# First norm of a two-layer backbone: leading weight tiles take x times the adaLN scale, with shift and rstd put in afterwards, and every engine in a written order

## The chip, the cores and the metric

The kernel runs on one core of one Trainium2 chip. The metric is the device time of one execution in microseconds (us), and what is compared is the median of several executions. The core has five engines that run side by side, each with its own queue of instructions that it works off in order: TensorE (PE, matrix products; PEld is its loading of weights), VectorE (DVE), ScalarE (ACT), GpSimd (POOL) and SyncE (SP, which here only starts transfers between HBM and the on-chip memory SBUF). Products are accumulated in eight PSUM banks. In this kernel an engine waits for another through semaphores.

## The reference, cut to what matters

The program is a two-layer transformer backbone in float32: two streams of 256 tokens each (latent x and context c), width 1024, each layer a SwiGLU FFN, an attention mixer and a second FFN, every one behind an RMS norm with adaLN (shift, scale, gate). Only the start of layer 0 is touched:

```python
cond_x = jax.nn.silu(c); cond_c = jax.nn.silu(c_ctx)
mx = jnp.split((cond_x @ mod_w[layer] + mod_b[layer])[:, None, :], N_MOD, axis=-1)   # mc with cond_c
y = xf * lax.rsqrt(jnp.mean(xf * xf, axis=-1, keepdims=True) + EPS)                    # rms_norm, then * norm_g
h = y * (1.0 + scale) + shift                                                         # modulate(h, mx[0], mx[1])
g, u = jnp.split(h @ w_in, 2, axis=-1)
return (jax.nn.silu(g) * u) @ w_out
```

Shift and scale are themselves products of a 1024 vector with a 1024x1024 block of `mod_w`, one pair for each stream.

## The kernel before, in words

Everything is held transposed: channels on the 128 partitions, both streams side by side in 512 columns, so x is eight blocks `xs[0..7]` of 128x512. A float32 product is made of three products of float32r halves: the operand is split into a high half (a cast on ACT, line 198) and a low half (a subtraction on DVE, line 199), and `mm3` (lines 226 to 228) adds high x high, high x low, low x high. A weight tile is 128x1024 (eight blocks k, for 128 output channels), so a tile takes 24 products of 128x512. For the FFN, tiles 2f and 2f+1 are the gate and the up part of hidden block f.

The first norm needs shift and scale at once. The matrix block for them is loaded as eight columns (`load_column`, 1 MB each in four transfers of 256 KB), each column with shift and scale of one k. `mod_sums` (line 143) makes 16 small float32 products for a column, ACT copies the result (149), PE turns it (151), and three short DVE instructions (158 to 160) make shift and `(1 + scale) * g`. With these `inputs(k)` makes the normed input of block k: for each stream x times coefficient times rstd on DVE (1049), high half plus shift on ACT (1051), low half on DVE (1052). rstd comes first of all, from the squares of the whole of x (1014, 1018, 1022, 1032, 1036, 1039). The four leading weight tiles (`sl.lead`) are multiplied block by block as the inputs come (`lead_products`); from tile 4 on `Sublayer.products` takes one tile after the other. `fill` (line 88) issues products of ones that nobody reads, 40 at the start and 3 and 5 while columns 0 and 1 are turned.

The order of the instructions on an engine comes from the framework that builds the program, which looks ahead by its own costs; `behind(x)` asks for a place after instruction x. The transfers stand in one SP queue: all of x, then the columns with the four weight tiles between them, then constants, then the first pieces of later work.

Next to the FFN, DVE works through the adaLN vectors of later sublayers (`mod_in_background`, lines 169 and 171: products of 128x1024 blocks with one number per partition, two per block), from hidden block 2 on.

## Time and profile before

| what | value |
|---|---|
| median of three executions | 1690.58 us (1689.67 to 1690.87) |
| profiled execution | 1692.26 us, span of the program in it 1690.5 us |
| PE busy | 1671.4 us, 99% of the span |
| DVE busy | 1076.8 us, 64% |
| ACT busy | 643.1 us, 38% |
| HBM read | 241.16 MB, 143 GB/s over the span |

The rows of the profile name the line of the kernel, engine, operation and tiles. In the timeline a row has the start and the duration in us, and `x4` means that four neighbouring instructions were merged into one row. In brackets stands how long the engine had been idle and what released it. A float32 product of PE shows as two records, so the 16 products of a column are x32. A product of 128x512 shows a duration of about 0.39 us, but the next one starts after 0.23 us, since products are pipelined.

### The profile page before, as it was taken

To read this page: it belongs to the slowest core of one execution; us is meant where nothing else is said; L and a number is where in the kernel's file an instruction comes from. 1 tells how busy PE (TensorE), PEld (TensorE's weight loads), DVE (VectorE), ACT (ScalarE), POOL (GpSimd) and SP (SyncE) were. 2 spreads that over 40 slices of the span, in tenths; PEclk is the share of its full clock that TensorE was granted. 3 is DMA by queue.
4 is the path that set the end of the run, shared out by engine and by line. 5 is a ranking of instruction groups with operands and counts; after the bars stand their busy time and mean duration, and the time that the engine had idled before them with its cause. 6 is when DMAs were issued, how large, how long until landed. Compare 5 with 4: busy or idle time off the path is not lost.

```text
span 1690.5 us, 23440 instructions
## 1 busy us (share of the span) xinstructions
PE 1671.4 (99%) x9294; PEld 1418.6 (84%) x9294; DVE 1076.8 (64%) x1535; ACT 643.1 (38%) x1129; POOL 231.1 (14%) x192
## 2 busy tenths in 40 slices
PE   9999999999999999999999999999999999999997
PEld 7888888888888898888888897888888898889997
DVE  6766687645667568856847365744433367777886
ACT  4421322235556353222222352222222357754444
POOL 0000000004133130000000130000000255132332
PEclk9999999999999999999999999999999999999999
DMA  9645455431211126644645335735332222245553
GB/s 344 221 164 183 166 189 198 159 121 63 88 51 63 63 83 200 204 150 158 205 146 173 106 112 199 238 115 165 114 104 90 98 88 77 71 154 178 173 186 113
DMA packets 71535, 243.75 MB, mean 144 GB/s; under 512 B 8576, under 2 KB 9344, under 8 KB 71424
## 3 DMA queue, kind: packets, MB, share of 16 engines
q1 hardware_dynamic: 70560, 241.54, 43.3%
q8 instruction: 73, 1.20, 0.3%
q10 hardware_dynamic: 864, 0.70, 0.1%
q14 instruction: 38, 0.31, 0.1%
HBM read 241.16 MB, written 1.05 MB: 143 GB/s over the span
## 4 chain that ended last, share of the span: by engine, by line
PE 86%; DMA 5%; POOL 3%; DVE 3%; ACT 2%; issue 1%; ACTq 0%; SPq 0%; DVEq 0%; POOLq 0%
PE bank L226 26%; PE bank L227 26%; PE bank L228 25%; DMA wraw<-in_woutn 3%; POOL wraw L962 3%; DVE wlo L199 2%; ACT whi L198 1%; DMA r2k<-in_modo 1%; PE bank L811 1%; PE bank L842 1%; PE bank L829 1%; PE bank L177 1%; PE bank L956 1%; PE bank L512 1%; PE bank L239 0%
## 5 line engine op out<-in xcount | busy, mean ns | idle before, releaser
L226 PE MATMUL bank<-r2k,whi 128*128 128x512 f32 (+2 forms) x2410 | 859.6, 358 | 0.9 <-ACT small L968 0.9
L227 PE MATMUL bank<-r2k,whi 128*128 128x512 f32 (+2 forms) x2410 | 854.7, 355 | 1.9 <-DVE r2k L202 1.2
L228 PE MATMUL bank<-r2k,wlo 128*128 128x512 f32 (+2 forms) x2410 | 854.3, 355 | 1.1 <-DVE wlo L199 0.9
L198 ACT CAST whi<-wraw 128x1024 fp32r<-128x1024 f32 (+1 forms) x308 | 316.9, 1033 | 840.1 <-PE bank L227 492.5
L226 PEld LDWEIGHTS bank<-r2k,whi 128*128 128x128 f32 x2410 | 455.4, 189 | 79.3 <-ACT whi L198 9.2
L227 PEld LDWEIGHTS bank<-r2k,whi 128*128 128x128 f32 x2410 | 456.3, 189 | 66.7 <-DVE r2k L202 1.9
L228 PEld LDWEIGHTS bank<-r2k,wlo 128*128 128x128 f32 x2410 | 456.2, 189 | 65.5 <-DVE wlo L199 2.0
L199 DVE TENSOR_TENSOR wlo<-wraw,whi 128x1024 fp32r<-128x1024 f32 (+1 forms) x297 | 358.4, 1213 | 109.8 <-ACT whi L198 102.4
L171 DVE SCALAR_TENSOR_TENSOR big<-modraw,conds,big 128x1024 f32<-128x1024 f32 x189 | 233.6, 1280 | 9.5 <-DMA modraw<-in_modw 8.6
L264 POOL TENSOR_TENSOR strip<-strip 128x256 f32<-128x256 f32 x58 | 56.3, 984 | 935.8 <-ACT strip L258 465.6
L366 DVE SCALAR_TENSOR_TENSOR x<-bank,mod,x 128x256 f32<-128x256 f32 x168 | 74.4, 479 | 151.3 <-PE bank L228 149.7
L458 DVE TENSOR_TENSOR tmp<-bank,tmp 128x512 f32<-128x512 f32 x66 | 45.6, 691 | 160.8 <-PE bank L228 158.3
L962 POOL TENSOR_TENSOR wraw<-wraw,gate 128x1024 f32<-128x1024 f32 x22 | 62.1, 2821 | 130.9 <-DMA wraw<-in_woutn 115.3
L956 PE MATMUL bank<-whi,r2k 128*128 128x512 f32 x176 | 58.2, 393 | 3.1 <-DVE r2k L977 1.8
L199 DVE TENSOR_TENSOR r2k<-bank,r2k 128x512 fp32r<-128x512 f32 (+2 forms) x73 | 40.5, 593 | 18.9 <-ACT r2k L198 18.6
L977 DVE TENSOR_TENSOR r2k<-tmp,r2k 128x256 fp32r<-128x256 f32 x22 | 46.6, 2118 | 0.9 <-ACT r2k L976 0.9
L199 DVE TENSOR_TENSOR r2k<-tmp,r2k 128x512 fp32r<-128x512 f32 x66 | 45.2, 685 | 1.4 <-ACT r2k L198 1.4
L198 ACT CAST r2k<-tmp 128x512 fp32r<-128x512 f32 x66 | 41.0, 622 | 11.3 <-DVE tmp L458 11.0
L484 DVE TENSOR_REDUCE small<-bank 128x1 f32<-128x512 f32 (+1 forms) x64 | 37.2, 616 | 10.6 <-PE bank L816 10.3
L956 PEld LDWEIGHTS bank<-whi,r2k 128*128 128x128 f32 x176 | 33.0, 188 | 10.1 <-DVE r2k L977 2.2
L456 ACT ACTIVATE tmp<-bank 128x512 f32<-128x512 f32 x66 | 38.9, 590 | 3.7 <-PE bank L228 3.7
L198 ACT CAST r2k<-bank 128x512 fp32r<-128x512 f32 (+2 forms) x73 | 34.5, 524 | 15.0 <-PE bank L228 9.7
(203 smaller groups left out, 1199.0 us busy)
## 6 DMA issues: line engine op xcount, KB each, us to landing
wraw<-in_win SPq DMA_DIRECT2D x172, 512.0 KB, 3.6
modraw<-in_modw SPq DMA_DIRECT2D x128, 512.0 KB, 4.1
wraw<-in_wout SPq DMA_DIRECT2D x48, 448.0 KB, 3.4
wraw<-in_wout SPq DMA_DIRECT2D x24, 512.0 KB, 4.3
wraw<-in_woutn SPq DMA_DIRECT2D x22, 512.0 KB, 3.5
r2k<-in_modo SPq DMA_DIRECT2D x32, 256.0 KB, 6.0
wraw<-in_mwo SPq DMA_DIRECT2D x8, 512.0 KB, 3.6
wraw<-in_swq SPq DMA_DIRECT2D x8, 512.0 KB, 3.4
```

Of the source, the lines that this page charges most:

```text
L171: nc.vector.scalar_tensor_tensor(acc[s], raw, conds[:, kt, s:s + 1], acc[s], ALU.mult, ALU.add)
L198: nc.scalar.copy(hi, src)
L199: return engine.tensor_tensor(lo, src, hi.bitcast(F32), ALU.subtract)
L226: nc.tensor.matmul(o, lhsT=ah, rhs=bh, start=(i == 0), stop=False)
L227: nc.tensor.matmul(o, lhsT=ah, rhs=bl, start=False, stop=False)
L228: nc.tensor.matmul(o, lhsT=al, rhs=bh, start=False, stop=(i == n - 1))
L264: nc.gpsimd.tensor_tensor(self.parts[0], self.parts[0], q, ALU.add)
L366: nc.vector.scalar_tensor_tensor(xs[d][:, SL[s]], o[:, SL[s]], mod[l][:, s, c:c + 1], xs[d][:, SL[s]], ALU.mult, ALU.add)
L458: nc.vector.tensor_tensor(pr[:, :w], ou[:, :w], sg[:, :w], ALU.mult)
L956: nc.tensor.matmul(acc[i][h], lhsT=gu[a][:, rows], rhs=w[b][:, cols], start=(f == 0 and j == 0), stop=(f == NF - 1 and j == 2))
L962: nc.gpsimd.tensor_tensor(raw, raw, gate, ALU.mult)
L977: nc.vector.tensor_tensor(gu[1], u, gu[0].bitcast(F32), ALU.subtract)
```

## The change

The transfers now stand in this order: x blocks 0 and 1, the scale of columns 0 and 1, two weight tiles; then for each pair of blocks x, scale columns and (twice) a weight tile; then the shift columns pair by pair, with weight tiles 4 and 5 between them. So scale and shift of a pair of columns are two sums of 16 products each in place of two mixed ones: eight sums as before. The result is turned by a product with a 128x4 matrix (`both_halves`) that also adds the halves, in place of a transposition and a DVE addition.

The four leading tiles take z = x times `(1 + scale) * g`, split into halves (`gained_high` on ACT, `gained_low` on DVE): without rstd and without shift. What is missing is put in for hidden blocks 0 and 1: the PSUM result is multiplied by rstd (a factor of each token), and the product of the weight tile with the shift vector (`ends`, 32 small products on PE, a copy, a transposition) is added, in `silu` as its bias and in the up part as a scalar. The normed inputs themselves (`scaled`, `halves`) are still made for the later tiles, after rstd; tiles 4 and 5 (`more`) are multiplied with them. Squares, sums, leading products and inputs are written out in one order, and `queued` holds each of PE, ACT and DVE to that order: an instruction of this stage is placed behind the last one of the stage on its engine. All these instructions carry the line of `queued`, 1035.

```diff
-    for d in range(0, KT, 2):
+    def load_x(d):
         nc.sync.dma_start(x_all[:, d:d + 2], t["xT"][:, d:d + 2])
+    load_x(0)
...
+                if sl.ends is not None and f < 2:
+                    nc.vector.tensor_tensor(sg, og, sl.rstds, ALU.mult)
+                    nc.vector.tensor_tensor(pr, ou, sl.rstds, ALU.mult)
+                    for s in streams:
+                        nc.scalar.activation(sg[:, SL[s]], sg[:, SL[s]], AF.Silu, bias=sl.ends[:, 2 * f, s:s + 1])
+                        nc.vector.scalar_tensor_tensor(pr[:, SL[s]], pr[:, SL[s]], sl.ends[:, 2 * f + 1, s:s + 1], sg[:, SL[s]],
+                                                       ALU.add, ALU.mult)
+                else:
+                    nc.scalar.activation(sg[:, :w], og[:, :w], AF.Silu)
+                    nc.vector.tensor_tensor(pr[:, :w], ou[:, :w], sg[:, :w], ALU.mult)
...
+    scales.append(load_columns(0, 1))
+    load_weight()
+    load_weight()
+    for k in range(2, KT, 2):
+        load_x(k)
+        scales.append(load_columns(k, 1))
+        if k < 6:
+            load_weight()
+    for k in range(0, KT, 2):
+        shifts.append(load_columns(k, 0))
+        if k < 4:
+            more.append(weight_raw(*ffn_specs(0, 0)[len(more) + 4]))
...
+    def queued(engine, f, *args, **kw):
+        with behind(last.get(engine)):
+            last[engine] = f(*args, **kw)
+        return last[engine]
...
+    def gained_low(d):
+        z = zs[d]
+        for s in range(2):
+            dve(nc.vector.scalar_tensor_tensor, z[1][:, SL[s]], xs[d][:, SL[s]], sl.gain(s, d), z[0][:, SL[s]].bitcast(F32),
+                ALU.mult, ALU.subtract)
...
+    sA = sums(scales[0])
+    weight_high(wraws[0], sl.lead)
+    idle(6)
+    v = turn(sA)
+    idle(8)
+    scale_of(0, v)
+    gained_high(0)
+    gained_low(0)
+    weight_low(wraws[0], sl.lead[0])
...
+    sA = sums(scales[3])
+    lead_products((3,), (4,))
+    v = turn(sA)
+    scale_of(6, v)
+    lead_products((3,), (5,))
+    for k in (6, 7):
+        gained_high(k)
+        gained_low(k)
+    sA = sums(shifts[0])
+    scaled(0)
+    lead_products(range(4), (6,))
+    v = turn(sA)
+    shift_of(0, v)
+    scaled(1)
+    sA = sums(shifts[1])
+    weight_high(more[0], more)
+    halves(0)
+    scaled(2)
+    halves(1)
+    weight_low(more[0], more[2])
+    lead_products((0, 1), (7,))
+    v = turn(sA)
+    shift_of(2, v)
+    sA = sums(shifts[2])
+    scaled(3)
+    halves(2)
+    weight_high(more[1], more)
+    scaled(4)
+    halves(3)
+    weight_low(more[1], more[3])
+    del more[:2]
+    lead_products((2, 3), (7,))
+    v = turn(sA)
+    shift_of(4, v)
+    sA = sums(shifts[3])
+    scaled(5)
+    halves(4)
+    scaled(6)
+    halves(5)
+    v = turn(sA)
+    shift_of(6, v)
...
+    def products_of_inputs():
+        for k in range(KT):
+            for wt, o, M in more:
+                mm3(o, sl.terms(wt, M, slice(0, TT)), (k,), KT)
...
+        for k in range(KT):
+            for j in range(4):
+                nc.tensor.matmul(b[32 * j:32 * j + 32, :P], lhsT=shift32[:, k], rhs=wraws[j][:, k * P:(k + 1) * P],
+                                 start=(k == 0), stop=(k == KT - 1), skip_group_check=True)
```

How this stands on the engines, at three places. First PE, from the last column before and from the last shift sum now. In the rows, `32x128 x16` is a sum, `128x512` a product of a weight tile; before:

```order
L143 MATMUL bank<-r2k,cond_124 32x128 x16
L226 MATMUL bank<-r2k,whi 128x512
L227 MATMUL bank<-r2k,whi 128x512
L151 MATMUL bank<-c_ident,tmp 128x128
L228 MATMUL bank<-r2k,wlo 128x512
L226 MATMUL bank<-r2k,whi 128x512
```

Now (`both_halves` is the turning product; the rows of line 1035 end with it, and those of line 217 are tiles 4 and 5):

```order
L1035 MATMUL bank<-both_halves,tmp 128x4
L1035 MATMUL bank<-r2k,cond_121 32x128 x16
L1035 MATMUL bank<-r2k,whi 128x512 x2
L1035 MATMUL bank<-r2k,wlo 128x512
L1035 MATMUL bank<-r2k,whi 128x512 x2
L1035 MATMUL bank<-r2k,wlo 128x512
L1035 MATMUL bank<-both_halves,tmp 128x4
L1035 MATMUL bank<-r2k,cond_121 32x128 x16
L1035 MATMUL bank<-both_halves,tmp 128x4
L217 MATMUL bank<-r2k,whi 128x512
```

Before, products of leading tiles stand between the last sum and its turning product, and go on behind it. Now nothing stands between the last shift sum and its turning product, and all 48 products of tiles 4 and 5 stand behind it.

Second ACT, at the same place. `COPY tmp<-bank 128x128` is the copy of a sum that the turning product waits for, `ACTIVATE r2k<-strip` the high half of a normed input. Before:

```order
L149 COPY tmp<-bank 128x128
L1051 ACTIVATE r2k<-strip,mod_127 128x256 x2
L198 CAST whi<-big 128x1024
L149 COPY tmp<-bank 128x128
L1051 ACTIVATE r2k<-strip,mod_127 128x256 x2
L149 COPY tmp<-bank 128x128
```

Now, from the split of weight tile 4 on:

```order
L1035 CAST whi<-wraw 128x1024
L1035 ACTIVATE r2k<-strip,mod_124 128x256 x4
L1035 COPY tmp<-bank 128x128
L1035 ACTIVATE r2k<-strip,mod_124 128x256 x2
L1035 CAST whi<-wraw 128x1024
L1035 ACTIVATE r2k<-strip,mod_124 128x256 x2
L1035 COPY tmp<-bank 128x128
L189 CAST whi<-wraw 128x1024 x2
```

The copy of the last shift sum stands behind the high halves of inputs 0 to 3 and the high halves of weight tiles 4 and 5, and the high halves of tiles 6 and 7 follow it at once.

Third DVE, from the turning of the first shift pair on. `strip<-x` is x times coefficient times rstd of one stream, `r2k<-strip` a low half, `mod_124<-bank` the shift of a pair:

```order
L1035 TENSOR_TENSOR mod_124<-bank,c_modb 128x2x2
L1035 SCALAR_TENSOR_TENSOR strip<-x,coefA_126,r2k 128x256 x2
L1035 SCALAR_TENSOR_TENSOR r2k<-strip,mod_124,r2k 128x256 x2
L1035 SCALAR_TENSOR_TENSOR strip<-x,coefA_126,r2k 128x256 x2
L1035 SCALAR_TENSOR_TENSOR r2k<-strip,mod_124,r2k 128x256 x2
L1035 TENSOR_TENSOR wlo<-wraw,whi 128x1024
L1035 TENSOR_TENSOR mod_124<-bank,c_modb 128x2x2
L1035 SCALAR_TENSOR_TENSOR strip<-x,coefA_126,r2k 128x256 x2
```

Before, the DVE work of an input stood right behind the coefficient of its own column:

```order
L158 TENSOR_TENSOR mod_127<-bank,c_modb 128x2x2
L159 TENSOR_TENSOR mod_127<-bank,mod_127 128x2x2
L160 SCALAR_TENSOR_TENSOR coefA_129<-mod_127,c_ng 128x2
L1049 SCALAR_TENSOR_TENSOR strip<-x,coefA_129,strip 128x256 x2
L1052 SCALAR_TENSOR_TENSOR r2k<-strip,mod_127,r2k 128x256 x2
```

Now the shift of the second pair stands behind the low halves of the first pair and behind the low half of weight tile 4. All inputs stand behind the 16 low halves of z.

## Prediction

> **What bounds the kernel now.** I read the page first, then the timeline, groups and waits of the first 100 us, where the change is.

> ```profile
> span 1690.5 us, 23440 instructions
> PE 1671.4 (99%) x9294; PEld 1418.6 (84%) x9294; DVE 1076.8 (64%) x1535; ACT 643.1 (38%) x1129; POOL 231.1 (14%) x192
> ```

> PE sets the time. A change can win only PE's waits and its work that no result needs, and it loses whatever wait it puts on PE. The start, in the timeline:

> ```profile
> 1.04 11.66 PE L88 MATMUL bank<-ones 128*128 128x128 f32 x80 [1.04 <-DVE ones L79]
> 12.54 0.95 PE L1022 MATMUL bank<-ones,tmp 128*128 128x1 f32 x8
> 13.42 1.08 PE L143 MATMUL bank<-r2k,cond 128*32 128x128 f32 x32
> 14.43 0.65 PE L1036 MATMUL bank<-c_ident,small 128*128 128x128 f32 x4
> 14.59 0.27 ACT L149 COPY tmp<-bank 128x128 f32<-128x128 f32 x1 [0.80 <-PE bank L143]
> 14.92 0.32 PE L151 MATMUL bank<-c_ident,tmp 128*128 128x128 f32 x1
> 18.12 1.28 PE L88 MATMUL bank<-ones 128*128 128x128 f32 x10
> 19.16 0.48 PE L226 MATMUL bank<-r2k,whi 128*128 128x512 f32 x1
> ```

> The 40 products of ones hold PE until 12.5 us; they stay. The first product of a weight tile starts at 19.16. Then the groups of PE from 19.0 to 52.6 us, and what PE waited for in 12 to 53:

> ```profile
> L226 PE MATMUL bank<-r2k,whi 128*128 128x512 f32 x33 | 13.7, 424 | 0.0
> L227 PE MATMUL bank<-r2k,whi 128*128 128x512 f32 x33 | 13.0, 395 | 0.0
> L228 PE MATMUL bank<-r2k,wlo 128*128 128x512 f32 x32 | 12.6, 405 | 0.0
> L143 PE MATMUL bank<-r2k,cond 128*32 128x128 f32 x192 | 8.1, 277 | 1.0 <-DMA r2k<-in_modo 0.9
> PE bank L143 <- DMA r2k<-in_modo: 1.1, 3, 0.6
> ```

> 98 products have started by 52.6: the 96 of the four leading tiles, and two of tile 4. The waits for columns are 1.1 us in all. How far apart PE starts products, and what a sum costs it:

> ```profile
> 56.46 0.39 PE L226 MATMUL bank<-r2k,whi 128*128 128x512 f32 x1
> 82.30 0.39 PE L226 MATMUL bank<-r2k,whi 128*128 128x512 f32 x1
> 37.43 0.39 PE L228 MATMUL bank<-r2k,wlo 128*128 128x512 f32 x1
> 37.75 1.08 PE L143 MATMUL bank<-r2k,cond 128*32 128x128 f32 x32
> 38.76 0.50 PE L226 MATMUL bank<-r2k,whi 128*128 128x512 f32 x1
> 39.10 0.40 PE L227 MATMUL bank<-r2k,whi 128*128 128x512 f32 x1
> ```

> Between the first two rows lie 38 blocks of three products: 25.84 / 114 = 0.227 us each. From 37.43 to 39.10 two products and a sum are started: 1.67 - 0.45 = 1.2 us for a sum. My yardstick is the end of tile 5, the 144th product. Before it is 52.2 + 48 x 0.227 = 63.1, and 63.2 with a short wait for the low half of tile 4.

> **Does the bound move at all?** PE's own work to that point, from 12.5 us on. Before: 144 products 32.7, eight sums 9.6, eight turnings 1.2 (0.15 each, see below), 0.95 + 0.65 for rstd, eight products of ones 2.1 (1.28 / 5 = 0.257 each): 47.2, so 3.5 of the 50.7 us were waits. Now: the same 32.7, 9.6, 1.2 and 1.6, 18 products of ones 4.6, and the shift product with its turning, 32 small products of a sum's shape, so two sums 2.4, plus 0.2: 52.3. So even if every wait vanished, the end would be at 64.8, 1.6 us later than before. The new load order removes 1.1 us of waits; the rest of the 3.5 is paid back in products of ones and the shift product. A gain is nearly excluded by this, and the question is which waits the written order adds.

> **The prices** of what the new order chains, from the timeline (two streams are two instructions, so half of an x2 row each):

> ```profile
> 6.30 5.46 DVE L1018 TENSOR_TENSOR tmp<-tmp 128x512 f32<-128x512 f32 x7
> 15.28 0.17 DVE L158 TENSOR_TENSOR mod<-bank,c_modb 128x4 f32<-128x4 f32 x1 [1.27 <-PE bank L151]
> 17.80 0.91 ACT L1051 ACTIVATE r2k<-strip,mod 128x256 fp32r<-128x256 f32 x2
> 18.34 0.88 DVE L1052 SCALAR_TENSOR_TENSOR r2k<-strip,mod,r2k 128x256 fp32r<-128x256 f32 x2 [0.38 <-ACT r2k L1051]
> 21.06 1.03 ACT L198 CAST whi<-big 128x1024 fp32r<-128x1024 f32 x1
> 22.12 1.23 DVE L199 TENSOR_TENSOR wlo<-big,whi 128x1024 fp32r<-128x1024 f32 x1 [0.45 <-ACT whi L198]
> ```

> DVE starts its low half at 18.34, 0.08 after ACT's first high half (17.80 + 0.455): I take 0.07 for a handover. `gained_high`, `scaled` and `gained_low` have the shapes of these rows and get their prices; as new forms they may be off by some per cent, which moves no term by over 0.5 us. A turning product with four columns lies between 0 and the 0.32 of line 151; I take 0.15.

> **To the first product:** sum 12.5 to 13.7, six products of ones to 15.25 (the copy needs 0.4 of that), turning, eight of ones to 17.46. The first product starts 1.7 us earlier than before.

> **17.5 to 43.9**, up to the turning of the last scale pair. 69 products 15.7, three sums 3.6, four products of ones 1.0, two turnings 0.3, totals and rstd transpositions 1.9: 22.5. Waits: the third product needs weight 0's low half, which stands on DVE behind the two low halves of block 0, 0.8; then 0.4 for block 1. When the third scale pair is turned PE has no products left, and waits through two coefficients, two ACT halves and three handovers, 1.6 + 0.3. Totals wait 0.4 for the last square sums. With two of 0.2, 3.9 in all: 43.9. DVE is idle for 5.3 us before this turning, since PE has not got to it, although all its inputs after it are still to be made.

> **Transfers are off the path:**

> ```profile
> 0.00:10.00 10.00, 8.96 (x58) 8.96 (x59) 3.95 (x10) 5.92 (x10) 0.19 (x4) 1.00 0.84 303
> 20.00:30.00 10.00, 9.01 (x117) 6.16 (x117) 7.28 (x20) 5.19 (x11) 0.00 (x0) 1.00 1.05 391
> ```

> The last number is GB/s: 3.0 MB by 10 us, then 0.39 MB per us. The scale pairs end at 1.7, 4.4, 6.5 and 8.6 MB of the new order and the shift pairs at 9.6, 11.2, 12.8 and 13.8, so the last one comes at about 38.8 with its latency. PE asks for the scale sums at 12.5, 20.1, 28.1, 41.8, for the shift sums at 44.6, 48.7, 51.4, 54.1: each is there by then.

> **43.9 to 59.8, the new wait.** PE: 18 products 4.1, two sums 2.4 and a turning bring the last product of tile 0 to its end at 50.7 (DVE by then has done the last four low halves of z and the scaled inputs 0 and 1). Now ACT's high half of tile 4 may overwrite tile 0's buffer: 50.7 + 1.03 = 51.8. High half of input 0, stream one, and handover: 52.3. DVE: low halves 0, scaled 2, low halves 1 (3 x 0.88), low half of tile 4 (1.23), shift of pair two (0.19): 56.4. ACT: high halves 2 (0.91), tile 5 (1.03), high halves 3 (0.91), and only then the copy of the last shift sum (0.27): 59.6. PE turns it and starts tile 4 at 59.8. In the meantime PE had three products of tile 1, six of tiles 2 and 3, two sums and two turnings, and was through at 55.3: it stands still for 4.3 us. Before, products stood between sum and turning.

> **59.8 to 73.6.** 48 products 10.9 and 0.3 for tile 5's low half: 71.0. The halves of inputs 4 to 7 come in time (DVE ends them at 68.9, PE asks for block 7 at 69.6), by under 1 us. The shift product takes 2.4 and its turning 0.2; the copy between them (0.27 and two handovers) lies beside two products of tile 6: 73.6. Late: 73.6 - 63.2 = 10.4 us.

> **The first hidden blocks.** DVE has this behind it, and the background:

> ```profile
> 53.33 0.69 DVE L458 TENSOR_TENSOR tmp<-bank,tmp 128x512 f32<-128x512 f32 x1 [0.69 <-ACT tmp L456]
> 55.14 0.68 DVE L199 TENSOR_TENSOR r2k<-tmp,r2k 128x512 fp32r<-128x512 f32 x1
> 57.74 1.41 DVE L169 TENSOR_SCALAR big<-modraw,conds 128x1024 f32<-128x1024 f32 x2
> 59.06 2.48 DVE L171 SCALAR_TENSOR_TENSOR big<-modraw,conds,big 128x1024 f32<-128x1024 f32 x2
> wraw<-in_win SPq DMA_DIRECT2D x172, 512.0 KB, 3.6
> ```

> Blocks 0 and 1 cost it 4 x 0.69 + 4 x 0.44 in place of 2 x 0.69: 3.1 us more. The low halves of tiles 7, 8, 9 end at 74.3, blocks 0 to 2 at 81.1; with the background between them, the low halves of tiles 10, 11, 12 at 93.3, 100.2, 107.1. PE wants them at 95.9, 101.3 and 106.8 (5.45 a tile from 73.6, and 0.5 into it): tile 12 is 0.3 late. Bounds 0 and 3, since three such places follow each other with under 3 us to spare; I take 0.5. Later the order of every engine is the same as before, and PE stays the bound.

> **Sum:** 10.4 + 0.5 = 10.9 us on a span of 1690.5, so 1701.4. The profiled execution took 1692.26 around that span; the median of the runs is 1690.58, 0.1 from the span: 1701.5 for the median.

> **Rivals.**

> *Waits hidden, no loss.* The chain through ACT and DVE would run beside PE's products, and only PE's work counts: 64.8 for 63.2, 1692. For it: the stage has products enough (144) and 99% PE; against it: the rows of the order leave none between last sum and turning. It decides if the last copy is done by 55.2 in place of 59.6. 7%. A real gain (under 1687.2) would need PE to have less work than reckoned: 3%.

> *Half of it.* The waits of 17 to 44 us (3.9) don't come, and the chain starts that much earlier against a PE that is earlier too, or its prices are smaller: 1695 to 1698, 14%.

> *The DVE backlog grows.* Each transfer of the background waits for a buffer that DVE frees, 3.6 us each as in the row above; if DVE falls 2 us further behind, the low halves of tiles 10 to 12 each delay PE: 3 to 5 more, 1704.5 to 1706.5. 13%.

> *A slow clock after the standstill.* The source view of line 88 has durations as minimum/median/maximum:

> ```profile
> L88 PE MATMUL bank<-ones x96: 274/275/582, 1.0 to 19.1; 128*128 128x128 f32 x96
> ```

> The first products of ones take twice as long; 80 records take 11.66, at 0.128 they would take 10.2: 1.4 us lost at the cold start. If a standstill of 4.3 us brings that back, it is 1702.9. For it: the longest wait of this stage before is 0.6, so the trace never tried it; against it: its granted clock is 1.00 in every window. 13%. [...]

> **How the numbers follow.** The forecast, 1698.5 to 1704.5, has 50%, and with the clock, inside it, 63%. 1696 to 1706 leaves out the hidden waits and the gain (10%), a part of "half of it" (5%) and of the backlog (4%). What a measurement here can tell from no change is 0.2%, 3.4 us: slower by more 90%, within 7%, faster 3%.

> **What would show it.** Right: the first tile product at about 17.5; a PE wait of 3 to 6 us for the copy before the last turning near 55 to 60, with ACT and DVE busy in it; tile 5 ended at about 71; no waits of PE for columns. Wrong: products running through 55 to 60, or the leading tiles done before 50; a PE wait on shift columns; a slower granted clock there.

## The result, and the profile after

The changed kernel takes 1702.91 us in the median of four executions (1700.55 to 1703.66) against 1690.72 of the kernel before beside it: ratio 1.0064 with a 95% interval of 1.0052 to 1.0076, so it is slower, by more than the 0.2% that a measurement can tell. In a second set it took 1701.38 (1700.01 to 1705.45, five executions) against 1691.33: 1.0063, 1.0050 to 1.0076. The profiled execution of the first set is its fastest, 1700.55 us with a span of 1698.7.

The page's first rows, and the timeline of PE at the start and around the last turning (start, duration, engine, line, operation; in brackets the idle time before and what ended it):

```profile
span 1698.7 us, 23648 instructions
PE 1675.3 (99%) x9387; PEld 1422.1 (84%) x9387; DVE 1074.9 (63%) x1550; ACT 649.5 (38%) x1147; POOL 229.1 (13%) x192
```

```profile
11.72 1.08 PE L1035 MATMUL bank<-r2k,cond 128*32 128x128 f32 x32
...
16.10 0.77 PE L1035 MATMUL bank<-r2k,whi 128*128 128x512 f32 x2
...
52.41 1.08 PE L1035 MATMUL bank<-r2k,cond 128*32 128x128 f32 x32
56.81 0.59 PE L1035 MATMUL bank<-both_halves,tmp 128*128 128x4 f32 x2 [3.32 <-ACT tmp L1035]
57.26 0.77 PE L217 MATMUL bank<-r2k,whi 128*128 128x512 f32 x1
57.83 0.63 PE L218 MATMUL bank<-r2k,whi 128*128 128x512 f32 x1
58.26 0.63 PE L219 MATMUL bank<-r2k,wlo 128*128 128x512 f32 x1
...
62.45 0.40 PE L217 MATMUL bank<-r2k,whi 128*128 128x512 f32 x1
62.69 0.40 PE L218 MATMUL bank<-r2k,whi 128*128 128x512 f32 x1
...
70.42 0.39 PE L219 MATMUL bank<-r2k,wlo 128*128 128x512 f32 x1
70.74 1.95 PE L1254 MATMUL bank<-big,gate 128*32 128x128 f32 x64
72.63 0.50 PE L217 MATMUL bank<-r2k,whi 128*128 128x512 f32 x1
```

Between the last shift sum (52.41) and its turning (56.81) PE stands still for 3.32 us, waiting for ACT's copy. And what follows is slow: from 57.26 to 62.1 the products start 0.43 us apart, and only then 0.23. Tile 5, the yardstick, ends at 70.65 (its last product starts at 70.42, and the next could start 0.23 later) where it ended at 63.2. The waits of PE between 12 and 120 us (total, times, longest):

```profile
PE bank L1035 <- ACT tmp L1035: 3.3, 1, 3.3
PE bank L1035 <- ACT r2k L1035: 1.4, 1, 1.4
PE bank L1035 <- DVE wlo L1035: 0.6, 1, 0.6
```

None is for columns (before, three of them, 1.1 us), and none lies behind the standstill. ACT in it:

```profile
53.96 0.91 ACT L1035 ACTIVATE r2k<-strip,mod 128x256 fp32r<-128x256 f32 x2 [2.40 <-DVE mod L1035]
54.77 1.03 ACT L1035 CAST whi<-wraw 128x1024 fp32r<-128x1024 f32 x1
55.71 0.90 ACT L1035 ACTIVATE r2k<-strip,mod 128x256 fp32r<-128x256 f32 x2
56.52 0.24 ACT L1035 COPY tmp<-bank 128x128 f32<-128x128 f32 x1
```

The sum is done at 53.5, but the copy stands behind three items of ACT, and the first of these waits for DVE's third shift pair (`mod`), on which DVE comes only at 53.76. The granted clock of the same stretch, from the view by windows (window, its length, busy us and instructions of PE, PEld, DVE, ACT, POOL, granted clock, DMA share, GB/s); the windows are cut where the granted clock changes:

```profile
48.70:52.12 3.42, 3.42 (x45) 2.81 (x44) 1.88 (x5) 2.81 (x6) 0.00 (x0) 1.00 0.00 0
52.12:55.53 3.41, 1.37 (x36) 1.04 (x34) 3.41 (x9) 1.57 (x3) 0.00 (x0) 1.00 0.17 34
55.53:58.94 3.41, 2.13 (x6) 1.84 (x7) 3.41 (x8) 3.41 (x7) 0.00 (x0) 0.50 0.35 127
58.94:62.36 3.42, 3.42 (x9) 2.65 (x9) 3.42 (x8) 1.37 (x4) 0.00 (x0) 0.50 0.76 232
62.36:65.77 3.41, 3.41 (x16) 2.79 (x16) 3.41 (x11) 2.14 (x5) 0.00 (x0) 1.00 0.50 171
```

A stretch in which PE worked 1.37 of 3.41 us is followed by two at half the clock. So the rival of the slow clock came true, beside the wait. From here on the difference stays. The first residual row of the first FFN on DVE (source view; the line is 366 before and 358 now; minimum, median and maximum of its duration, then first and last start) is 9.9 us later, and the last 9.8:

```profile
L366 DVE SCALAR_TENSOR_TENSOR x<-bank,mod,x x168: 469/478/488, 126.9 to 1484.5; 128x256 f32<-128x256 f32 x168
```

```profile
L358 DVE SCALAR_TENSOR_TENSOR x<-bank,mod,x x168: 470/477/486, 136.8 to 1494.3; 128x256 f32<-128x256 f32 x168
```

### The profile page after: what moved, and what is told of

Same layout as the page of the kernel before. It is cut to its first block, busy times and chain, and to the rows that moved or that the text cites. A ratio compares the mean times of both kernels' runs of the same rounds, so it can differ in the third digit from the quotient of the medians.

```text
span 1698.7 us, 23648 instructions
## 1 busy us (share of the span) xinstructions
PE 1675.3 (99%) x9387; PEld 1422.1 (84%) x9387; DVE 1074.9 (63%) x1550; ACT 649.5 (38%) x1147; POOL 229.1 (13%) x192
## 3 DMA queue, kind: packets, MB, share of 16 engines
HBM read 241.16 MB, written 1.05 MB: 143 GB/s over the span
## 4 chain that ended last, share of the span: by engine, by line
PE 84%; DMA 5%; POOL 3%; DVE 3%; ACT 2%; issue 2%; SPq 0%; ACTq 0%; DVEq 0%; POOLq 0%
PE bank L217 25%; PE bank L218 25%; PE bank L219 25%; DMA wraw<-in_woutn 4%; POOL wraw L962 3%; DVE wlo L190 2%; ACT whi L189 1%; PE bank L1035 1%; PE bank L811 1%; PE bank L842 1%; PE bank L829 1%; PE bank L168 1%; DMA r2k<-in_modo 1%; PE bank L512 1%; PE bank L230 0%
## 5 line engine op out<-in xcount | busy, mean ns | idle before, releaser
L217 PE MATMUL bank<-r2k,whi 128*128 128x512 f32 (+2 forms) x2378 | 846.3, 357 | 1.4 <-ACT small L968 1.4
L218 PE MATMUL bank<-r2k,whi 128*128 128x512 f32 (+2 forms) x2378 | 841.6, 354 | 1.9 <-DVE r2k L193 1.2
L219 PE MATMUL bank<-r2k,wlo 128*128 128x512 f32 (+2 forms) x2378 | 841.5, 354 | 1.1 <-DVE wlo L190 0.9
L189 ACT CAST whi<-wraw 128x1024 fp32r<-128x1024 f32 (+2 forms) x306 | 314.3, 1033 | 832.8 <-PE bank L218 493.2
L217 PEld LDWEIGHTS bank<-r2k,whi 128*128 128x128 f32 x2378 | 448.7, 189 | 78.0 <-ACT whi L189 8.4
L218 PEld LDWEIGHTS bank<-r2k,whi 128*128 128x128 f32 x2378 | 449.4, 189 | 65.5 <-DVE r2k L193 1.9
L219 PEld LDWEIGHTS bank<-r2k,wlo 128*128 128x128 f32 x2378 | 449.3, 189 | 65.0 <-DVE wlo L190 2.2
L190 DVE TENSOR_TENSOR wlo<-wraw,whi 128x1024 fp32r<-128x1024 f32 (+2 forms) x295 | 355.5, 1212 | 122.7 <-ACT whi L189 115.7
L358 DVE SCALAR_TENSOR_TENSOR x<-bank,mod,x 128x256 f32<-128x256 f32 x168 | 74.3, 478 | 150.2 <-PE bank L219 148.6
L458 DVE TENSOR_TENSOR tmp<-bank,tmp 128x512 f32<-128x512 f32 x64 | 44.2, 690 | 154.2 <-PE bank L219 152.9
L956 PEld LDWEIGHTS bank<-whi,r2k 128*128 128x128 f32 x176 | 33.0, 188 | 10.2 <-DVE r2k L977 2.2
L977 DVE TENSOR_TENSOR r2k<-tmp,r2k 128x256 fp32r<-128x256 f32 x22 | 40.0, 1819 | 0.9 <-ACT r2k L976 0.9
## 6 DMA issues: line engine op xcount, KB each, us to landing
wraw<-in_win SPq DMA_DIRECT2D x172, 512.0 KB, 3.6
modraw<-in_modw SPq DMA_DIRECT2D x128, 512.0 KB, 4.2
wraw<-in_wout SPq DMA_DIRECT2D x24, 512.0 KB, 4.3
wraw<-in_woutn SPq DMA_DIRECT2D x22, 512.0 KB, 3.5
wraw<-in_mwo SPq DMA_DIRECT2D x8, 512.0 KB, 3.4
wraw<-in_swq SPq DMA_DIRECT2D x8, 512.0 KB, 3.5
```

The source lines that it names most:

```text
L189: nc.scalar.copy(hi, src)
L190: return engine.tensor_tensor(lo, src, hi.bitcast(F32), ALU.subtract)
L217: nc.tensor.matmul(o, lhsT=ah, rhs=bh, start=(i == 0), stop=False)
L218: nc.tensor.matmul(o, lhsT=ah, rhs=bl, start=False, stop=False)
L219: nc.tensor.matmul(o, lhsT=al, rhs=bh, start=False, stop=(i == n - 1))
L358: nc.vector.scalar_tensor_tensor(xs[d][:, SL[s]], o[:, SL[s]], mod[l][:, s, c:c + 1], xs[d][:, SL[s]], ALU.mult, ALU.add)
```

## The experiments

All edits are relative to the changed kernel unless a heading says otherwise. Since everything of the change lies ahead of the first residual row, I read that row (the **landmark**) in each profile, with the stretches of half clock, and the medians beside it. The runs were taken in three sets, each with the kernel before beside it. The changed kernel itself was taken again only in the set of three of the edits (ones in the standstill, last sum moved, 28 products at the start); for the others the ratios to the kernel before are what can be compared.

### The changed kernel again

No edit.

> The changed kernel itself again, beside the others on one chip. All theories expect 1.005 to 1.0075 of the kernel before (1699.5 to 1703.5). Theory on the half clock: its profile shows the slow stretch right behind the standstill again, at 55 to 63 us. Rival (an accident of one execution): no slow stretch there, or at another place.

Measured: ratio 1.0063 (1.0050 to 1.0076). Its profile, windows cut in the same manner:

```profile
29.11:32.52 3.41, 1.99 (x9) 1.39 (x8) 1.60 (x6) 1.81 (x5) 0.00 (x0) 1.00 1.04 389
32.52:35.94 3.42, 3.42 (x10) 2.63 (x9) 2.87 (x5) 3.37 (x5) 0.00 (x0) 0.50 1.04 391
...
56.42:59.83 3.41, 1.07 (x6) 0.94 (x7) 3.41 (x8) 3.41 (x7) 0.00 (x0) 1.00 0.50 156
59.83:63.24 3.41, 3.41 (x10) 2.63 (x9) 3.41 (x8) 2.48 (x5) 0.00 (x0) 0.50 0.43 154
63.24:66.66 3.42, 3.42 (x17) 2.79 (x16) 3.42 (x11) 1.71 (x4) 0.00 (x0) 1.00 0.72 243
```

The slow stretch is back behind the standstill, once and not twice, and a second one came behind the wait of 1.4 us for the third scale pair, where the first profile had none. So it is no accident, but where it falls and how often differs from execution to execution. Landmark 138.5.

### PE kept at work in the standstill

```diff
     sA = sums(shifts[3])
+    idle(13)
     scaled(5)
```

> Thirteen products of ones (0.257 us each, 3.3 us, read by nobody) are put on TensorE between the last shift sum and its turning, so that it works through the standstill of 3.3 us; the turning itself still waits for the copy of line 1035 at about 56.8 us. Theory (half clock after the standstill): the products of tiles 4 and 5 start 0.23 us apart from the first one on, where the changed kernel has them 0.43 us apart from 57.3 to 62.1; tile 5 ends at 68.5 and not at 70.7, and the time is 2 us under the changed kernel's, about 1700.8, ratio 1.0055 to 1.006 to the kernel before against 1.0064 or more. Rival (the slow stretch is an accident of the profiled execution, or it comes from the long load of DVE and ACT): the same spacing of 0.43 us, or the time within 0.5 us of the changed kernel's 1702.9. Second rival (the copy is done earlier than the page tells, and the products of ones delay the turning): 1 to 3 us slower than the changed kernel.

Measured: no half clock from 10 to 75 us, tile 5 ends at 67.95 (68.5 expected), landmark 134.1. That is the theory, by the profile. By the time it isn't settled: 1701.52 us (1699.78 to 1703.01), ratio 1.0057 (1.0045 to 1.0070) against 1.0063 (1.0050 to 1.0076) of the changed kernel on the same chip; the intervals overlap. Its profile loses two stretches late, at 1506 to 1513 us. So I closed the other wait of this stage as well.

### PE kept at work in both waits

```diff
     lead_products((2,), (2, 3))
     v = turn(sA)
+    idle(5)
...
     sA = sums(shifts[3])
+    idle(13)
```

> Products of ones (read by nobody) stand in both long waits of PE: 13 between the last shift sum and its turning, and 5 between the turning of the third scale pair and the next products of tiles, where PE waits 1.4 us for ACT. Both lie in waits, so that no result comes earlier or later by them. Theory (PE at work less than about half in a stretch of 3.41 us brings half the clock in the next one): the profile has no half clock between 10 and 75 us, the first residual row of DVE starts at 133.5 to 134.8 (136.8 and 138.5 in the two profiles of the changed kernel), and the time is 2 to 2.5 us under the changed kernel on the mean, 1699 to 1700, if the late stretches at about 1505 and 1675 us fall as they did. Rival (the half clock comes by chance, whatever PE does): a stretch of half clock within 10 to 75 us, or the residual row at 136 and later.

Measured: 1699.96 us, and five executions within 1699.02 to 1700.48, where the changed kernel spread over 1700.01 to 1705.45. Ratio 1.0052 (1.0038 to 1.0066). Landmark 134.2, and the windows at the two waits:

```profile
28.29:31.70 3.41, 3.23 (x19) 2.53 (x18) 1.18 (x5) 1.66 (x5) 0.00 (x0) 1.00 1.00 359
31.70:35.12 3.42, 3.41 (x16) 2.76 (x16) 2.87 (x6) 3.40 (x5) 0.00 (x0) 1.00 0.99 350
...
52.18:55.60 3.42, 3.42 (x54) 3.20 (x53) 3.42 (x9) 1.67 (x3) 0.00 (x0) 1.00 0.22 40
55.60:59.01 3.41, 3.19 (x20) 2.66 (x19) 3.41 (x8) 3.41 (x8) 0.00 (x0) 1.00 0.30 121
```

The turning starts at 56.78 as before, so the products of ones changed no result's time; the 48 products of tiles 4 and 5 take 11.0 us (57.0 to 68.0) in place of 13.4 (57.26 to 70.65). The standstill's clock costs 2.4 us in the first profile and 1.6 in the second (59.0 to 71.6, one stretch). The intervals of the ratios still overlap, so that the clock is lost there and kept with the ones is shown by the profiles, and its size in the median (1.4 us between two sets) is not settled.

### The last shift sum ahead of ACT's and DVE's work

```diff
     sA = sums(shifts[2])
+    sB = sums(shifts[3])
...
     shift_of(4, v)
-    sA = sums(shifts[3])
+    v = turn(sB)
...
-    v = turn(sA)
     shift_of(6, v)
```

> The sum of the last shift pair is issued right behind that of the third one, so that ACT copies it ahead of the high halves of inputs 2 and 3 and of tile 5, and it is turned right behind the third shift. Nothing else is moved. Theory (the standstill is the copy's place in ACT's order, which waits for DVE): no wait of PE for a copy over 1.5 us after 50 us, tile 4 starts at 52 to 54 us and not at 57.3, and its inputs' low halves on DVE, which end at about 65, set the end of tile 5: about 66.5 us in place of 70.7. With the half clock gone too, 4 us under the changed kernel: 1698.9, range 1697.5 to 1700. Rival (DVE's load sets the start of tile 4 whatever the order): tile 5 ends later than 69.5 and the time is within 1 us of 1702.9. Under neither is it as fast as the kernel before (1690.7).

Measured: 1699.06 us, ratio 1.0044 (1.0031 to 1.0056), 2.3 us under the changed kernel beside it, though the intervals of the two ratios still overlap. The standstill is gone: the last two turnings stand side by side, and the longest wait behind them is 0.4 us, now for DVE:

```profile
55.88 0.50 PE L1035 MATMUL bank<-both_halves,tmp 128*128 128x4 f32 x4
56.24 0.49 PE L217 MATMUL bank<-r2k,whi 128*128 128x512 f32 x1
...
61.13 0.50 PE L219 MATMUL bank<-r2k,wlo 128*128 128x512 f32 x1 [0.41 <-DVE wlo L1035]
```

This profile began 1.3 us later (first sum at 13.01 for 11.72) and lost one stretch at 34.3 to 37.8, 1.6 us; less these 2.9 us, an estimate, tile 4 starts at 53.3 and tile 5 ends at 66.1, as the theory expected; as measured, 56.24 and 69.0, both missed it. That the copy's place in ACT's order made the standstill is shown. The gain is smaller than the 3.3 us it lasted, since DVE's halves come next.

### 28 products of ones at the start, in both kernels

```diff
-    fill(40)
+    fill(28)
```

> The products of ones at the start are 28 and not 40 (read by nobody), the rest stays. Theory (after the change nothing that PE needs first is as late as the end of these products: the scale columns of the first pair and the condition are there by about 9.5 us): the first sum starts at 8.6 to 10 us in place of 11.7, the first tile product at 14 to 15 in place of 16.1, and the end of tile 5 moves by 1 to 2.5 us; 1700.5 to 1702. Rival (the chain from the last product of tile 0 through ACT and DVE to the last copy is bound by DVE's own sum of work or by the loads, not by PE): the first product is earlier, but the last turning stays at 56.5 to 57.0 and the time stays within 0.5 us of the changed kernel's 1702.9.

> The kernel before with 28 products of ones at the start in place of 40. Theory (before the change the squares of all eight blocks end on DVE at about 12 us, and the totals need them, so that the 12 products stand in a wait): the first sum of squares' product starts at 11.8 to 12.5 as before, PE waits 2 to 3 us from about 9.5 on; no gain, within 0.7 us of the kernel before, or 1 to 2 us slower where the idle stretch brings half the clock. Rival (the 40 products at the start held the kernel before too): 1.5 to 3 us faster than the kernel before, as it is for the changed kernel.

Measured, changed kernel: 1698.45 us, ratio 1.0044 (1.0031 to 1.0058), 2.9 under the changed kernel beside it: more than the theory's 1 to 2.5, with intervals that overlap. In the profile the same work starts and ends earlier, the first sum at 10.11 for 11.72, the last turning at 55.40 for 56.81, with the same standstill of 3.32. Measured, kernel before: 1692.73, ratio 1.0012 (1.0003 to 1.0021), 1.2 us slower. There the 12 products stood in a wait for DVE's sum of squares, which now shows, and half the clock follows it:

```profile
11.90 1.05 PE L1022 MATMUL bank<-ones,tmp 128*128 128x1 f32 x8 [3.00 <-DVE tmp L1018]
```

```profile
10.71:14.12 3.41, 2.00 (x27) 1.60 (x31) 1.21 (x3) 1.13 (x3) 0.00 (x0) 1.00 1.00 361
14.12:17.54 3.42, 3.42 (x32) 2.87 (x24) 0.90 (x5) 1.55 (x4) 0.00 (x0) 0.50 1.04 398
```

Its landmark is the 126.9 us of the kernel before, and this execution is the fastest of the eleven; so what makes the median 1.2 us slower this profile doesn't show. The change did open a gain at the start (1.6 us at the first sum, 1.2 at the landmark), by taking the squares off the path, and left it unused behind products that were sized for the old start.

### No products of ones among the leading tiles

```diff
-    idle(6)
     v = turn(sA)
-    idle(8)
...
-    idle(4)
```

> The 18 products of ones that the changed kernel puts into its first 21 us (6, 8 and 4 of them, 0.257 us each, 4.6 us in all, read by nobody) are left out, the 40 at the start stay. Theory (they mostly stand where PE would wait for the copy and the first coefficients, so that they are no price of the change): the first tile product starts 0.8 to 1.5 us earlier, PE's waits before 35 us grow by 2 to 3 us, and the time is 0 to 1.5 us under the changed kernel run beside it; if stretches of 3.41 us in which PE works less than half bring half the clock, one such stretch can come at 13 to 20 us and take 1 to 1.7 us back. Rival (PE's own work sets the time, as the sum of 52.3 us in the prediction has it): the whole 4.6 us come off, tile 5 ends about 66 us and the time falls by 3.5 us or more.

Measured: 1701.21 us, ratio 1.0057 (1.0044 to 1.0069): no gain that can be told from the changed kernel's 1.0063 in the other set. PE's work is 4.6 us less. Some 2.1 of them come back as waits before 35 us (4.1 us for 2.0), as the theory had it, and two stretches of half clock take more:

```profile
13.29:16.70 3.41, 1.62 (x24) 0.92 (x16) 1.47 (x5) 2.82 (x7) 0.00 (x0) 1.00 1.05 413
16.70:20.11 3.41, 2.92 (x17) 1.50 (x20) 3.41 (x5) 2.02 (x4) 0.00 (x0) 0.50 1.04 395
20.11:23.53 3.42, 3.42 (x34) 2.69 (x27) 0.81 (x2) 0.27 (x1) 0.00 (x0) 0.50 1.03 399
```

The rival, by which PE's own work sets the time, is not borne out: tile 5 ends at 72.85 and not at 66. What these products of ones bought here was less waiting and the clock.

### 28 of the 32 shift products left out

```diff
-        for k in range(KT):
+        for k in range(1):
```

> Leaves out part of the computation: of the shift product (32 small products of four weight tiles with the shift) only the first four are made, so what is added to the first two hidden blocks is not the right sum. Theory (PE is the bound from the end of tile 5 on, and nothing hides these products): 28 of 32 small products at 1.9 / 32 = 0.059 us each, 1.7 us, come off; 1.7 us under the changed kernel (1.2 to 2.2). Rival (the low halves of tiles 7 to 12 on DVE or the background catch up and take their place): under 0.5 us, with new PE waits on low halves between 80 and 110 us.

Measured: 1702.27 us, ratio 1.0067 (1.0055 to 1.0080): no gain. The theory missed. At the place itself the time does come off: the first product of a tile behind them starts 0.36 us after the first shift product and not 1.89, and tile 6 is 1.7 us earlier. But the landmark is 136.5 against 136.8. Of this 0.9 us were given back at one sum of the background. The rows show PE's wait for it between 103 and 107 us, and the sum itself, here and then in the changed kernel:

```profile
PEld bank L168 <- DVE big L162: 1.1, 2, 0.8
```

```profile
103.87 1.99 PE L168 MATMUL bank<-big,ones 128*32 128x512 f32 x8
```

```profile
105.62 1.06 PE L168 MATMUL bank<-big,ones 128*32 128x512 f32 x8
```

PE comes to the first sum of the background (line 168) and finds DVE at its last product (162). In the changed kernel that one ended at 103.1 and PE asked at 105.6; here it ended at 104.8 and PE asked at 103.9. From there on PE stays 0.8 us ahead of the changed kernel to 139 us; the landmark, a row of DVE, is only 0.3 ahead, and at the last residual row nothing is left (1494.8 for 1494.3). Part of it is the experiment's own doing: the order of DVE is made by the framework from its own costs, and with a shorter product it put one low half of a weight more (1.22 us) ahead of the background. So this run doesn't say what the shift products cost at a fixed order; that stays open.

### Three edits together

28 products at the start, no products of ones among the leading tiles, and the last shift sum behind the third (the diffs above).

> Three edits together: 28 products of ones at the start in place of 40, no products of ones among the leading tiles, and the sum of the last shift pair right behind that of the third with its turning behind the third shift. Theory (the gains are of different waits and add up until DVE's work for the inputs of tiles 4 and 5 sets the end): no standstill over 1.5 us after 45 us, the low halves end at 61 to 63, tile 5 at 63 to 65; 1695 with a range of 1692.5 to 1697.5, so still 1 to 6 us over the kernel before. Rival 1 (PE's work sets it): tile 5 ends before 61.5 and the time is at or under the kernel before. Rival 2 (the waits that the products of ones filled bring stretches of half clock at 10 to 35 us, 1.7 us each): 1697.5 to 1700.

Measured: 1696.59 us, ratio 1.0029 (1.0019 to 1.0039). The time lies in the theory's range, 1.6 us over its figure, and the profile shows the theory's and rival 2's signs: no standstill, but PE worked 0.71 of the 3.41 us from 10.80 on, and 14.2 to 21.0 ran at half the clock. Tile 5 ends at 66.7 and not at 63 to 65; landmark 132.9.

### The edits that helped, with PE kept at work

28 products at the start, the last shift sum behind the third, `idle(5)` behind the turning of the third scale pair; the 18 products of ones stay.

> The edits that helped, with PE kept at work: 28 products of ones at the start in place of 40, the last shift sum right behind the third with its turning behind the third shift, and 5 products of ones in the wait behind the turning of the third scale pair; the 18 others stay. Theory (the gains add up and no stretch of half clock takes them back): no half clock in 10 to 75 us, tile 5 ends at 63.5 to 65, the first residual row starts at 130.5 to 132, the time is 1694.5 with a range of 1693 to 1696.5: 1 to 5 us over the kernel before. Rival (DVE's work sets the end whatever PE does before): tile 5 ends at 66 or later, the residual row at 133 or later, the time over 1696.5.

Measured: 1695.46 us (1693.28 to 1697.47, ten executions), ratio 1.0025 (1.0016 to 1.0034): the fastest version with the change, and still slower than the kernel before. No half clock in 10 to 75 us, tile 5 ends at 63.97:

```profile
L358 DVE SCALAR_TENSOR_TENSOR x<-bank,mod,x x168: 468/476/486, 130.3 to 1488.8; 128x256 f32<-128x256 f32 x168
```

Neither this profile nor the one with PE kept at work in both waits has a slow stretch in the stage, so they can be compared directly: first sum 2.3 us earlier (9.48 for 11.75), tile 5 4.05 earlier. So, taking the earlier start to carry through, 1.8 us are the standstill's worth, of 3.3 that it lasted; the rest of it turned into small waits for halves between 53 and 57 us. Against the kernel before 3.4 us remain at the landmark: 0.7 at the last product of tile 5 (63.74 for 63.03), 2.0 for the shift products, 0.2 for their turning, and 0.5 at the first sum of the background (line 168), which takes 1.57 us and not 1.06 since it waits for DVE. At the last residual row it is 4.3 us, and in the medians 4.7.

### Two low halves on POOL

As the version before (it is what the expectation calls the version with three edits), and the low halves of tiles 4 and 5 on the idle POOL:

```diff
+        if pool:
+            nc.gpsimd.tensor_tensor(lo, raw, hi.bitcast(F32), ALU.subtract)
+            return
```

> As the version with three edits, and the low halves of tiles 4 and 5 are made by POOL (its rows of this shape take 2.4 us) and not by DVE (1.22 us each), which idles there. Theory (behind the standstill DVE's work for tiles 4 and 5 is the bound): tile 5 ends 1.5 to 2.5 us earlier than in the version without POOL, the residual row starts at 128.5 to 130.5, the time is 1692.5 with a range of 1691 to 1694.5. Rival 1 (PE is the bound there already): no change against the version without POOL. Rival 2 (POOL's 2.4 us come late, or slow DVE's rows): a PE wait for the low half of tile 4 over 1 us and a time 0.5 to 2 us over the version without POOL.

Measured: 1698.35 us, ratio 1.0043 (1.0030 to 1.0055): 2.9 us slower than without POOL, more than rival 2 gave it. POOL and DVE:

```profile
48.56 2.39 POOL L1102 TENSOR_TENSOR wlo<-wraw,whi 128x1024 fp32r<-128x1024 f32 x1 [48.13 <-ACT whi L1035]
55.24 2.64 POOL L1102 TENSOR_TENSOR wlo<-wraw,whi 128x1024 fp32r<-128x1024 f32 x1 [4.29 <-ACT whi L1035]
```

```profile
48.92 2.71 DVE L1035 SCALAR_TENSOR_TENSOR r2k<-strip,mod,r2k 128x256 fp32r<-128x256 f32 x2 [2.21 <-ACT r2k L1035]
51.55 0.87 DVE L1035 SCALAR_TENSOR_TENSOR strip<-x,coefA,r2k 128x256 f32<-128x256 f32 x2
...
55.61 2.95 DVE L1035 SCALAR_TENSOR_TENSOR r2k<-strip,mod,r2k 128x256 fp32r<-128x256 f32 x2
```

Two DVE instructions that take 0.88 us elsewhere take 2.71 while POOL subtracts, and the next ones are as short as ever. So DVE lost 1.8 us (and 2.1 at the second place) to save 1.22 each. The first DVE pair ends at 51.6, 0.7 us after POOL (51.0), and the second at 58.6, again 0.7 us after it (57.9), as if most of its 0.88 us had still been to do. By what POOL's work holds DVE's up, the runs don't show.

Not all of the 3.1 us at the landmark (133.4 for 130.3) is POOL's, though. In this profile PE also waited for a column in its second sum, long before POOL starts, and tile 4 starts 0.9 us late; the other 2.2 come behind it, with a wait for POOL's second low half:

```profile
17.71 1.06 PE L1035 MATMUL bank<-r2k,cond 128*32 128x128 f32 x26 [0.27 <-DMA r2k<-in_modo]
...
57.93 0.50 PE L219 MATMUL bank<-r2k,wlo 128*128 128x512 f32 x1 [1.53 <-POOL wlo L1102]
```

Rival 2 is right in kind; the wait over 1 us stands at tile 5's low half and not at tile 4's.

### The stage and the rest, in all profiles

Landmark, stretches of half clock of 3.41 us in the stage (10 to 75 us) and later (up to 1685 us), and what is left of the span behind the landmark:

| profile | landmark | in the stage | later | rest |
|---|---|---|---|---|
| before | 126.9 | 0 | 2 | 1563.6 |
| before, 28 at the start | 126.9 | 1 | 0 | 1561.7 |
| changed | 136.8 | 2 | 0 | 1561.9 |
| changed, again | 138.5 | 2 | 2 | 1565.2 |
| ones in the standstill | 134.1 | 0 | 2 | 1564.2 |
| ones in both waits | 134.2 | 0 | 2 | 1564.5 |
| last sum moved | 135.9 | 1 | 1 | 1562.5 |
| 28 at the start | 135.6 | 2 | 1 | 1562.2 |
| no ones among the tiles | 138.9 | 4 | 1 | 1562.3 |
| few shift products | 136.5 | 2 | 1 | 1562.7 |
| three edits | 132.9 | 2 | 1 | 1562.8 |
| best | 130.3 | 0 | 1 | 1562.7 |
| best, with POOL | 133.4 | 0 | 1 | 1562.3 |

The rest is 1561.7 to 1561.9 without a late stretch, 1562.2 to 1562.8 with one, and 1563.6 to 1565.2 with two. So behind the landmark the change costs little or nothing: 0.2 us between the two profiles without a late stretch, and up to the last residual row the best version goes from 3.4 to 4.3 us over the kernel before, the changed kernel from 9.9 to 9.8. What single executions differ by there goes mostly with the late stretches. That these make the whole spread of the times wasn't shown: of the other executions there is only a mean clock, and it doesn't always follow the time (of the changed kernel 1703.94 us with 0.997, 1700.01 with 0.996).

## Why the prediction was right, point by point

The forecast was 1701.5 within 1696 to 1706, slower; the medians are 1702.91 and 1701.38. The sum of 10.9 us stands against 9.9 at the landmark. (The spans of the two profiles differ by 8.2, since the one before has two late stretches and the one after none.) So the sum is off by 1.0 us, and two of its terms by more: 1.9 (the waits up to 43.9) and 2.5 (the 48 products).

- **The bound**: right. PE is busy for 99% as before, and only its waits and added work moved the time.
- **To the first product** (17.46): it came at 16.10. The first sum started at 11.72, 0.8 earlier than assumed, since PE had its full clock earlier in this execution (from 4.3 us on, and from 6.2 in the profile before); from the sum to the product 4.4 us passed, not 4.96.
- **17.5 to 43.9**: mis-sized in two terms that cancel. The waits were 2.0 us (0.6 and 1.4) and not 3.9: totals and the second weight never made PE wait. The work took 23.7 us (25.8 less 2.0) and not 22.5; about 0.7 of that are waits too, which don't show behind a product's 0.39 us: the products at 17.85, 22.51 and 31.27 stand 0.45 to 0.52 us ahead of the next one, which starts when DVE's low half ends. Scale pair 4 was turned at 41.88.
- **Transfers off the path**: right, PE waited for no column.
- **The new wait**: right in place, chain and cause. The last product of tile 0 was done at 48.7 (forecast 50.7), the copy at 56.8 (59.6): the chain took 8.1 us and not 8.9. PE stood 3.3 us and not 4.3. Moving the last sum showed the copy's place to be the cause.
- **59.8 to 73.6**: here the forecast chose the wrong side. Tile 5 ended at 70.65 for 71.0, but only since the early start and the slow clock cancel. The forecast priced the 48 products at 10.9 us and left the slow clock to a rival; they took 13.4, and 11.0 with PE kept at work. The argument against that rival, a granted clock of 1.00 in every window, was no evidence: the kernel before had no long wait in this stage, late in its own profile the half clock stands twice (1501 and 1669 us, so its trace had tried it), and the window of 0 to 10 us reads 1.00 though the products of ones start more slowly at its beginning (6 to 7 records per us from 2 to 6 us, 12 from 7 us on), since the profile has no record of the clock before 6.2 us. The rival's price, 1.4 us by the cold start, was too small: 1.6 to 2.4. The shift products took 2.0, not 2.4.
- **Low halves of the inputs**: they ended at 65.1 (68.9) and were in time.
- **First hidden blocks**: 0.5 us forecast. Between the end of the turning and the landmark some 0.3 came in, and no wait for a low half shows. That DVE is nonetheless close to PE there, the run with few shift products showed.
- **Half of it**: the waits of the first 44 us did come smaller, as this rival had it, 2.0 for 3.9; the time didn't follow, since the work there took 1.2 more and the clock 2.4.

So the median agrees to 1.4 us partly by luck: with PE kept at work in both waits the landmark was 7.3 us late (134.2 for 126.9), well below the forecast of 10.9, and the half clock made up for it. (The median of that version, 1699.96 us, still lies in the range.)

## What to carry to other kernels

Price a standstill of the engine that sets the time twice: for its length, and for the clock that it may lose behind it (here 3.3 us, and 1.6 to 2.4 more); where nothing useful can be moved in, work that nobody reads can fill the wait; here it delayed no result (the turning started at 56.78 for 56.81) and kept the clock (no half clock from 10 to 75 us). In an order written by hand look for a short instruction that the busiest engine waits for and that stands behind long ones on another engine, as the copy did; but count what its engine does next, since 3.3 us of standstill were worth 1.8. When a change takes something off the path at the start, look again at the fillers that were sized for it.
